# Gated MLP in three chunks of inner features, with seven block products for eight in five of eleven gate groups

## The chip, the cores and the metric

One core of one Trainium2 chip runs the kernel. The metric is device time in microseconds (us) for one execution. The kernel before was run three times: 2100.64 us is the median, 2100.33 the lowest and 2100.79 the highest. One further execution was profiled; its own time is 2100.51 us, and the span from its first to its last instruction is 2098.7 us.

In the profile, PE is the matrix engine (TensorE) and PEld its loads of the stationary operand. DVE is VectorE, ACT is ScalarE, POOL is GpSimd, and SP issues the DMAs. Each engine takes its own instructions in the order in which the program issues them.

## The reference

Two decoder layers on 256 tokens with 2048 features, all in float32. Layer 0 mixes tokens with MoBA attention, layer 1 with latent attention (MLA); each is followed by the gated MLP that the change is about:

```python
D_FF = 5632          # 44 tiles of 128 inner features
def conv_glu_ffn(h, w_gate, w_up, conv_w, conv_b, w_down):
    g = h @ w_gate                       # 256 x 2048 times 2048 x 5632
    g = causal_depthwise_conv(g, conv_w) + conv_b      # width 3 over tokens
    return (silu(g) * (h @ w_up)) @ w_down             # 5632 x 2048 back

x = x + mixer(rms_norm(x, attn_norm[i]))
x = x + conv_glu_ffn(rms_norm(x, ffn_norm[i]), ...)
```

(The convolution is written here as a function of that name; the reference calls a general one with one group per feature.)

## The kernel before

**Products in three parts.** Every weight is read as float32 and split into a high part, rounded to the matrix engine's format, and a low part that holds the rest. Activations are kept split in the same way. A product is then three matmuls: high by high, high by low, low by high (lines 261 to 263 in `feat_major`, line 235 in `tok_major`).

**Pieces and units.** A piece is 128 partitions by 512 weight columns. In the MLP a piece holds four tiles of 128 x 128, so 12 matmuls with 256 moving columns (the tokens). A unit is what one DMA brings, normally four pieces, 1 MB; three buffers named `raw` hold units. The list `units` fixes their order for the whole kernel. `Stream.split` makes the two parts of a piece: `whi` by a copy on ACT (line 104), then `wlo` by a subtraction on DVE (line 105). There are five buffers for each part.

**The order of the work is written out by hand.** `add` appends one quantum per piece. `at(q, f)` hangs a side step on quantum q, `first(q, f)` puts a step ahead of it. The loop at the end of `trunk` issues, for every q: the steps of `first`, then the splits up to piece q + 3, then the matmuls of piece q, then the side steps of q. So on DVE and on ACT the splits and the side steps stand in one line, and a side step that waits holds up every split behind it. Piece i can be split when piece i - 5 has left its buffer.

**The MLP before.** `plan_gate_up` goes through the 44 tiles of inner features; each tile is four gate pieces, then four up pieces. The side steps of a tile (class `FTile`) follow its gate product: `evac_gate` (DVE, line 675) takes it out of PSUM, `conv_last` (ACT, 682) and `conv_rest` (DVE, two operations of line 688) do the convolution, `silu` (ACT, 693), `scaled` (DVE, 696). After the up product come `product` (DVE, 699), `high` (ACT, 702) and `low` (DVE, 706), which leave the tile in `ffn["a"]`, with room for all 44. `plan_down_feat` then makes 16 output tiles of 11 pieces each, and `residual` (DVE, line 345) adds each to `xT`. After the down products of layer 0 the steps of the next norm hang on the same passes (lines 279, 284, 298, 302).

In `feat_major` the weight tile is stationary and the tokens move, so a result has features on partitions. In `tok_major` the activations are stationary and the weights move.

Of the kernel before, what the change touches and what calls it, by code (L numbers as in the profile page):

```python
# [10 lines left out]
F32 = mybir.dt.float32  # L11
F32R = mybir.dt.float32r
# [5 lines left out]
P = 128  # L18
# [30 lines left out]
BY_TOKEN, BY_FEATURE = (8, 8), (24, 56)  # L49

H_START = 8


class Stream:
# [3 lines left out]
    def __init__(self, nc, raw_pool, part_pool, units, starts):  # L58
        self.starts = starts
        self.nc, self.raw_pool, self.part_pool = nc, raw_pool, part_pool  # L60
        self.units = units
        self.pieces = [(u, i, n) for u, (_, k, n) in enumerate(units) for i in range(k)]
        self.raw, self.parts = {}, {}
        self.loaded = self.split_to = 0

    def load(self, upto):
        while self.loaded < min(upto, len(self.units)):
            u = self.loaded
            src, k, n = self.units[u]
            t = self.raw_pool.tile([P, 4 * 512], F32, name="raw")  # L70
            self.nc.sync.dma_start(t[:, : k * n], src)
            self.raw[u] = t
            self.loaded += 1

    def begin(self, load_x):

        ends = (2, 2, 3, 4, 6, 6, 8, 8, 10, 10, 13, 16)
        load_x(0, 1)
        at = 1
        for u in range(AHEAD_UNITS):  # L80
            src, k, n = self.units[u]
# [8 lines left out]
        self.loaded = AHEAD_UNITS  # L90

    def split(self, upto):
        while self.split_to < min(upto, len(self.pieces)):
# [3 lines left out]
            w = self.raw[u][:, j * n : (j + 1) * n]  # L97
            b, c = self.starts(u, j)
            hi = self.part_pool.tile([P, 512 + ROOM], F32R, name="whi")[:, b : b + 512]
            lo = self.part_pool.tile([P, 512 + ROOM], F32R, name="wlo")[:, c : c + 512]  # L100
            if i == 0:
                self.nc.vector.tensor_copy(hi[:, :n], w)
            else:
                self.nc.scalar.copy(hi[:, :n], w)  # L104
            self.nc.vector.tensor_tensor(  # L105
                lo[:, :n], w, hi[:, :n].bitcast(F32), op=ALU.subtract
            )
# [8 lines left out]
def trunk(ctx: ExitStack, tc: tile.TileContext, a, out):  # L116
# [14 lines left out]
    def units_of(name, n=512):  # L131
        w = a[name]
        return [(w[u], w.shape[2] // n, n) for u in range(w.shape[0])]

    def grouped(name, per, g):
        return units_of(name)[g * per : (g + 1) * per]
# [6 lines left out]
    units += units_of("ffn_gu0")  # L143
    units += units_of("ffn_down0")
    units += units_of("mla_wq_a")
    units += grouped("mla_wqr", 1, 0)
    units += units_of("mla_wkv_a", KVN)
# [6 lines left out]
    units += units_of("ffn_gu1")  # L154
    units += units_of("ffn_down1")
    def starts(u, j):

        return BY_TOKEN if u < 48 or 200 <= u < 222 else BY_FEATURE

    assert len(units) == 370  # L160
    ws = Stream(nc, raw_pool, part_pool, units, starts)
# [490 lines left out]
    def open_ffn(layer):  # L652
# [6 lines left out]
        ffn["a"] = ffn["pool"].tile([P, NF, 2 * S], F32R, name="a", bufs=1)  # L659
# [4 lines left out]
    class FTile:  # L664
        def __init__(self, layer, j, norm):
            self.layer, self.j, self.norm = layer, j, norm
            self.gate, self.up = {}, {}

# [32 lines left out]
        def high(self):  # L701
            nc.scalar.copy(ffn["a"][:, self.j, :S], self.c)

        def low(self):
            a_ = ffn["a"]
            nc.vector.tensor_tensor(
                a_[:, self.j, S:], self.c, a_[:, self.j, :S].bitcast(F32), op=ALU.subtract
            )

    def plan_gate_up(layer, norm):  # L710
        for j in range(NF):
            f = FTile(layer, j, norm)
            for kind, st in (("g", f.gate), ("u", f.up)):
# [3 lines left out]
                if kind == "g":  # L717
                    if j == 0:
                        at(q, open_ffn, layer)
                    at(q, f.evac_gate)  # L720
                    at(q + 1, f.conv_last)
                    at(q + 2, f.conv_rest)
                    at(q + 3, f.silu)
                    at(q + 4, f.scaled)
                else:
# [3 lines left out]

    plan_gate_up(0, n2)  # L730

    n3 = Norm(C_AN + KD, False)

    def plan_down_feat(norm):
        for j in range(KD):
            st = {}
            for kq in range(NF // 4):
                q = add(lambda t_hi, t_lo, n, st=st, kq=kq: feat_major(
                    st, lambda: ffn["a"], 4 * kq, NF - 1, kq == 0, t_hi, t_lo, n))
            at(q, residual, st, j, 0)  # L740
            if norm is None:
                at(q, store, j)
            elif j < KD - 1:
                norm.plan(q + 2, j)
            else:
                at(q, norm.now, j)
                at(q + 3, norm.sums)
        return q

    plan_down_feat(n3)  # L750
# [224 lines left out]
    plan_gate_up(1, n4)  # L975

    plan_down_feat(None)
# [125 lines left out]
```

## Time and profile before

| | us |
|---|---|
| median of three runs | 2100.64 |
| lowest, highest | 2100.33, 2100.79 |
| profiled execution, its own time | 2100.51 |
| its span | 2098.7 |
| PE busy in the span | 2090.2 |
| DVE busy | 1389.4 |
| ACT busy | 1134.2 |

How to read it: the span runs from the first to the last instruction. Busy time of an engine leaves out waits and the issuing of DMAs. Matmuls overlap, so the time that one takes (276 ns for 256 columns) is not the time from one to the next; that is read from the starts in the timeline. In a timeline row the columns are start, duration, engine, line, operation, output and inputs, count, and in brackets the idle time before it with what ended it. In a group row they are line, engine, operation, shapes and count, then total busy us and mean ns of one, then the idle time ahead.

Layer 0's MLP runs from about 393 to 1112 us of the span, and layer 1's from about 1376 us to the end.

### The profile page before, as it was taken

To read this page: it belongs to the slowest core of one execution; us is meant where nothing else is said; L and a number is where in the kernel's file an instruction comes from. 1 tells how busy PE (TensorE), PEld (TensorE's weight loads), DVE (VectorE), ACT (ScalarE), POOL (GpSimd) and SP (SyncE) were. 2 spreads that over 40 slices of the span, in tenths; PEclk is the share of its full clock that TensorE was granted. 3 is DMA by queue.
4 is the path that set the end of the run, shared out by engine and by line. 5 is a ranking of instruction groups with operands and counts; after the bars stand their busy time and mean duration, and the time that the engine had idled before them with its cause. 6 is when DMAs were issued, how large, how long until landed. Compare 5 with 4: busy or idle time off the path is not lost.

```text
span 2098.7 us, 42064 instructions
## 1 busy us (share of the span) xinstructions
PE 2090.2 (100%) x16684; PEld 2014.8 (96%) x16684; DVE 1389.4 (66%) x3036; ACT 1134.2 (54%) x2206; POOL 45.6 (2%) x37
## 2 busy tenths in 40 slices
PE   9999999999999999999999999999999999999999
PEld 7888889999999999999999889999999999999999
DVE  6776666766666766655556786767766667655554
ACT  6555555655555555545455675655555555544443
POOL 0000000000000000000000110000000000000000
PEclk9999999999999999999999999999999999999999
DMA  7444445555555555555554533545555555555553
GB/s 272 161 166 176 168 170 188 190 191 201 190 193 201 187 196 199 192 195 195 195 192 158 176 139 106 196 181 200 186 197 198 187 199 195 189 205 208 194 206 131
DMA packets 59381, 391.81 MB, mean 187 GB/s; under 512 B 6960, under 2 KB 10032, under 8 KB 13232
## 3 DMA queue, kind: packets, MB, share of 16 engines
q1 hardware_dynamic: 59040, 388.87, 52.3%
q8 instruction: 130, 2.13, 0.4%
q14 instruction: 67, 0.55, 0.1%
q10 hardware_dynamic: 144, 0.26, 0.1%
HBM read 387.01 MB, written 2.10 MB: 185 GB/s over the span
## 4 chain that ended last, share of the span: by engine, by line
PE 97%; DVE 1%; DMA 1%; issue 0%; ACT 0%; POOL 0%; SPq 0%; ACTq 0%; POOLq 0%
PE acc L261 26%; PE acc L263 26%; PE acc L262 26%; PE acc L235 15%; PE sc L473 1%; PE tp L449 1%; DMA raw<-in_moba_wq 1%; PE sc L520 1%; PE tp L509 0%; PE sc L476 0%; PE sc L521 0%; DVE wlo L105 0%; DMA xT<-in_xT 0%; DVE junk L379 0%; POOL hr L392 0%
## 5 line engine op out<-in xcount | busy, mean ns | idle before, releaser
L105 DVE TENSOR_TENSOR wlo<-raw,whi 128x512 fp32r<-128x512 f32 (+1 forms) x1480 | 1000.5, 684 | 424.6 <-ACT whi L104 422.5
L104 ACT CAST whi<-raw 128x512 fp32r<-128x512 f32 (+1 forms) x1479 | 871.8, 614 | 461.4 <-PE acc L262 213.6
L261 PE MATMUL acc<-h,whi 128*128 128x256 f32 x2880 | 795.3, 276 | 0.0
L263 PE MATMUL acc<-h,wlo 128*128 128x256 f32 x2880 | 794.9, 276 | 0.0
L262 PE MATMUL acc<-h,whi 128*128 128x256 f32 x2880 | 794.9, 276 | 0.0
L262 PEld LDWEIGHTS acc<-h,whi 128*128 128x128 f32 x2880 | 540.7, 188 | 0.0
L261 PEld LDWEIGHTS acc<-h,whi 128*128 128x128 f32 x2880 | 540.6, 188 | 0.0
L263 PEld LDWEIGHTS acc<-h,wlo 128*128 128x128 f32 x2880 | 540.6, 188 | 0.0
L261 PE MATMUL acc<-a,whi 128*128 128x256 f32 x1408 | 388.6, 276 | 0.0
L262 PE MATMUL acc<-a,whi 128*128 128x256 f32 x1408 | 388.6, 276 | 0.0
L263 PE MATMUL acc<-a,wlo 128*128 128x256 f32 x1408 | 388.6, 276 | 0.0
L235 PE MATMUL acc<-whi,h 128*128 128x512 f32 (+1 forms) x896 | 279.8, 385 | 0.7 <-ACT whi L104 0.5
L261 PEld LDWEIGHTS acc<-a,whi 128*128 128x128 f32 x1408 | 264.3, 188 | 0.0
L262 PEld LDWEIGHTS acc<-a,whi 128*128 128x128 f32 x1408 | 264.3, 188 | 0.0
L263 PEld LDWEIGHTS acc<-a,wlo 128*128 128x128 f32 x1408 | 264.3, 188 | 0.0
L235 PEld LDWEIGHTS acc<-whi,h 128*128 128x128 f32 x896 | 164.7, 188 | 31.5 <-ACT h L279 1.3
L235 PE MATMUL acc<-wlo,h 128*128 128x512 f32 (+1 forms) x448 | 169.3, 378 | 0.3 <-DVE wlo L105 0.2
L261 PE MATMUL acc<-oT,whi 128*128 128x256 f32 x512 | 144.8, 283 | 0.0
L263 PE MATMUL acc<-oT,wlo 128*128 128x256 f32 x512 | 141.7, 277 | 0.0
L262 PE MATMUL acc<-oT,whi 128*128 128x256 f32 x512 | 141.6, 277 | 0.0
L675 DVE TENSOR_TENSOR g<-acc,rstd_b 128x256 f32<-128x256 f32 x88 | 37.5, 426 | 126.0 <-PE acc L263 123.1
L682 ACT ACTIVATE c<-g,par 128x256 f32<-128x256 f32 x88 | 53.1, 603 | 108.1 <-DVE g L675 108.1
(141 smaller groups left out, 1558.0 us busy)
## 6 DMA issues: line engine op xcount, KB each, us to landing
raw<-in_ffn_gu SPq DMA_DIRECT2D x176, 1024.0 KB, 4.8
raw<-in_ffn_down SPq DMA_DIRECT2D x88, 1024.0 KB, 4.8
raw<-in_moba_wk SPq DMA_DIRECT2D x16, 1024.0 KB, 4.8
raw<-in_moba_wv SPq DMA_DIRECT2D x16, 1024.0 KB, 4.8
raw<-in_moba_wo SPq DMA_DIRECT2D x16, 1024.0 KB, 4.8
raw<-in_mla_wo SPq DMA_DIRECT2D x16, 1024.0 KB, 4.8
raw<-in_moba_wq SPq DMA_DIRECT2D x13, 1024.0 KB, 4.8
raw<-in_mla_wkv_a SPq DMA_DIRECT2D x8, 576.0 KB, 3.7
```

What stands on the lines that cost most here:

```text
L104: self.nc.scalar.copy(hi[:, :n], w)
L105: self.nc.vector.tensor_tensor(lo[:, :n], w, hi[:, :n].bitcast(F32), op=ALU.subtract)
L235: mm(state["acc"][t][:, :n], src[:, kt, c : c + P], (t_lo if part == 1 else t_hi)[:, :n], start=kt == 0 and part == 0, stop=kt == k_last a ...
L261: mm(o, w_hi, src[:, kt, :S], start=first and k == 0, stop=False, skip_group_check=True)
L262: mm(o, w_hi, src[:, kt, S:], start=False, stop=False, skip_group_check=True)
L263: mm(o, w_lo, src[:, kt, :S], start=False, stop=kt == k_last, skip_group_check=True)
L449: nc.tensor.transpose(tp[:, (i * NT + t) * P : (i * NT + t + 1) * P], flat[:, t, c : c + P], ident)
L473: mm(o, qT[:, i, q0 : q0 + P], kT[:, i, :n], start=True, stop=self.rope is None)
L520: mm(o[:, :S], v[:, 0, vs], self.pT[:, :S], start=True, stop=False)
L675: nc.vector.tensor_tensor(self.g[:, 2:], self.gate["acc"][:, :S], self.norm.rstd_b, op=ALU.mult)
L682: nc.scalar.activation(self.c, self.g[:, 2:], AF.Identity, bias=par[:, cb : cb + 1], scale=self.cw(2))
```

## The change

The MLP's 44 tiles are taken in three chunks: tiles 0 to 15, 16 to 31 and 32 to 43. After the gate and up products of a chunk, its down products are made at once: 16 passes of 4, 4 and 3 pieces, each with its own `residual`. `ffn["a"]` holds one chunk instead of 44 tiles.

For the five groups of four tiles named in `SUMS` (3, 4, 5, 8 and 9) the gate product is made by seven block products instead of eight. Tokens are cut into two halves and pairs of 128 input features into two, and the weights correspondingly; sums and differences of blocks are multiplied and combined. For a group there are four "sums" units, each of four tiles by 512 input features, and each unit is seven pieces of 6 matmuls with 256 moving weight columns and a stationary 128 x 128 block of activations. Four of the seven pieces of a unit are differences of weight blocks, made by `Stream.sum` on DVE in front of the split. The differences of the activations are made once per layer by `token_sums`, eight steps placed three pieces apart at the start of the MLP, and kept in `ffn["hs"]`. `joined` combines the seven results of a group, and `turned` brings each of its four tiles back to features on partitions by two transposes, just ahead of that tile's up pieces. The tile's steps from `evac_gate` to `scaled` then hang on the four up pieces.

The sums units of group 3 stand among the gate and up entries of the first chunk, one after every second tile; those of groups 4 and 5 stand among the down passes of chunk 0, and those of 8 and 9 among those of chunk 1, one after every second pass. The tiles 12 to 15, 16 to 23 and 32 to 39 thus have only up pieces in their place.

```diff
+CHUNKS = ((0, 16), (16, 32), (32, 44))
+SUMS = (3, 4, 5, 8, 9)
+def ffn_order():
+    order = []
+    def weave(plain, groups, begin, step):
+        sums = [("s", g, r) for g in groups for r in range(4)]
+        for i, p in enumerate(plain):
+            order.append(p)
+            if sums and i + 1 >= begin and (i + 1 - begin) % step == 0:
+                order.append(sums.pop(0))
+    for c, (j0, j1) in enumerate(CHUNKS):
+        plain = []
+        for j in range(j0, j1):
+            plain += [("p", j, kind) for kind in ("u" if j // 4 in SUMS else "gu")]
+        weave(plain, [3] if c == 0 else [], 8, 4)
...
+        weave([("d", c, j) for j in range(KD)], ahead, 2, 2)
...
+    def sum(self, upto):
+        while self.summed_to < min(upto, len(self.pieces)):
+            u, j, _ = self.pieces[self.summed_to]
+            self.summed_to += 1
+            if self.units[u][3] != "sums" or j in (0, 2, 4):
+                continue
+            if j == 3:
+                t = self.block(u, 1)
+                a, b = t, self.block(u, 0)
+            else:
+                t = self.sum_pool.tile([P, 512], F32, name="tsum", bufs=3)
...
+                if j == 1:
+                    a, b = self.block(u, 3), self.block(u, 1)
+                elif j == 5:
+                    a, b = self.block(u, 3), self.sums[u, 3]
+                else:
+                    a, b = self.block(u, 2), self.sums[u, 5]
+            self.sums[u, j] = t
+            self.nc.vector.tensor_tensor(t, a, b, op=ALU.subtract)
...
     def split(self, upto):
         while self.split_to < min(upto, len(self.pieces)):
...
             self.load(u + AHEAD_UNITS)
-            w = self.raw[u][:, j * n : (j + 1) * n]
+            self.sum(i + 1)
+            w = self.source(i)
...
-                self.nc.scalar.copy(hi[:, :n], w)
-            self.nc.vector.tensor_tensor(
-                lo[:, :n], w, hi[:, :n].bitcast(F32), op=ALU.subtract
-            )
+                self.nc.scalar.copy(w_hi, w)
+            if i + 1 < len(self.pieces) and self.pieces[i + 1][0] < self.loaded:
+                self.sum(i + 2)
+            self.nc.vector.tensor_tensor(w_lo, w, w_hi.bitcast(F32), op=ALU.subtract)
...
+    class Sums:
+        def work(self, norm, r, m, t_hi, t_lo, n):
...
+            for i in range(2):
...
+                mm(o, hi, w_hi, start=opens and i == 0, stop=False, skip_group_check=True)
+                mm(o, hi, w_lo, start=False, stop=False, skip_group_check=True)
+                mm(o, lo, w_hi, start=False, stop=last, skip_group_check=True)
+        def joined(self):
...
+            nc.scalar.copy(p1, w[:, :S])
...
+            add_(two(c[:, : 2 * S]), two(x[:, :]), twice(p1), op=ALU.add)
+            add_(two(f[:, :]), two(y[:, :]), twice(c[:, S : 2 * S]), op=ALU.add)
+            add_(c[:, 3 * S :], y[:, :S], f[:, S:], op=ALU.add)
+            add_(c[:, S : 3 * S], z[:, :], f, op=ALU.add)
+        def turned(self, tile_, i):
+            tile_.gate["acc"] = bank = ps_acc.tile([P, 512], F32, name="acc")
+            for t in range(NT):
+                at_ = t * 2 * S + i * P
+                nc.tensor.transpose(bank[:, t * P : (t + 1) * P], self.c[:, at_ : at_ + P], ident)
+    def token_sums(norm, pair):
...
+        for k in range(2):
+            c = norm.gain_col + 2 * pair + k
+            nc.scalar.activation(
+                x[:, k], xT[:, 2 * pair + k, :], AF.Copy, scale=par[:, c : c + 1]
+            )
...
+        sub(s_[:, 0], a21, a22, op=ALU.add)
+        sub(s_[:, 2], a11, a21, op=ALU.subtract)
+        sub(s_[:, 1], s_[:, 0], a11, op=ALU.subtract)
+        sub(s_[:, 3], a12, s_[:, 1], op=ALU.subtract)
...
+        nc.scalar.copy(hi, flat)
+        nc.vector.tensor_tensor(lo, flat, hi.bitcast(F32), op=ALU.subtract)
+    def plan_ffn(layer, norm, after):
...
+                for m in range(7):
+                    q = add(lambda t_hi, t_lo, n, grp=grp, r=r, m=m: grp.work(norm, r, m, t_hi, t_lo, n))
+                if r == 3:
+                    at(q, grp.joined)
...
+                    for pair in range(KD // 2):
+                        at(q + 4 + 3 * pair, token_sums, norm, pair)
+                if kind == "u" and j // 4 in SUMS:
+                    q0 = q - 4
+                    first(q0 + 1, groups[j // 4].turned, f, j % 4)
+                if kind == "g" or j // 4 in SUMS:
+                    at(q0, f.evac_gate) if kind == "g" else at(q0 + 1, f.evac_gate)
+                    at(q0 + 1, f.conv_last)
+                    at(q0 + 2, f.conv_rest)
+                    at(q0 + 3, f.silu)
+                    at(q0 + 4, f.scaled)
+                if kind == "u":
                     at(q, f.product)
                     at(q + 1, f.high)
                     at(q + 2, f.low)
```

The weights lie in memory as before. A sums unit is read as four runs of 2 KB per partition, and a down unit of a chunk by one or two DMAs of 1 to 4 pieces.

More of the change, by code (lines that the diff above doesn't have):

```diff
@@ L153, in trunk @@
     units += units_of("mla_wo")
[L154 to L161, printed above, removed]
+    units += ffn_units(1)
+    ws = Stream(nc, raw_pool, part_pool, units)
     att = ExitStack()
@@ L667, in __init__ @@
             self.gate, self.up = {}, {}
+            self.slot = j - max(j0 for j0, _ in CHUNKS if j0 <= j)
         def cw(self, i):
@@ L701, in high @@
         def high(self):
-            nc.scalar.copy(ffn["a"][:, self.j, :S], self.c)
+            nc.scalar.copy(ffn["a"][:, self.slot, :S], self.c)
         def low(self):
@@ L716, in plan_gate_up @@
                         st, lambda: norm.h, 4 * kq, KD - 1, kq == 0, t_hi, t_lo, n))
[L717 to L725, printed above, removed]
+                q0 = q
+                if kind == "g" and j == 0:
+                    at(q, open_ffn, layer)
+                    for pair in range(KD // 2):
[10 more added lines that the diff above has]
+                if kind == "u":
                     at(q, f.product)
```

177 lines of the change are left out of this document (135 added, 42 removed).

## Prediction

> **What bounds the kernel now.** I read the page first, then the matrix engine's share of the stretch that is layer 0's MLP, then the timeline of its matmuls, and last those of DVE and ACT in one tile, because the change trades matmuls for work there. The page, and the busy time of each engine from 393 to 1111 us:
>
> ```profile
> span 2098.7 us, 42064 instructions
> PE 2090.2 (100%) x16684; PEld 2014.8 (96%) x16684; DVE 1389.4 (66%) x3036; ACT 1134.2 (54%) x2206; POOL 45.6 (2%) x37
> PEclk9999999999999999999999999999999999999999
> ```
> ```profile
> core 0: us, PE busy (x) PEld busy (x) DVE busy (x) ACT busy (x) POOL busy (x), PEclk, DMA share, GB/s
> 393.00:1111.00 718.00, 718.00 (x6336) 717.90 (x6336) 470.52 (x845) 378.80 (x696) 1.08 (x1) 1.00 0.55 194
> ```
>
> PE is busy for 718.00 of 718.00 us there, at a granted clock of 1.00: no wait reaches it in the whole MLP. The pace is read from starts, here with 51 matmuls between the two rows:
>
> ```profile
> 600.05 0.28 PE L261 MATMUL acc<-h,whi 128*128 128x256 f32 x1
> ...
> 605.83 0.28 PE L261 MATMUL acc<-h,whi 128*128 128x256 f32 x1
> ```
>
> 5.78 / 51 = 113.3 ns. A piece of 12 matmuls is 1.36 us, four pieces 5.44, a sums piece of six 0.68. DVE's 66% looks like room, but a share hides the order. This is a tile before the change, first DVE, then ACT:
>
> ```profile
> 703.95 0.42 DVE L675 TENSOR_TENSOR g<-acc,rstd_b 128x256 f32<-128x256 f32 x1 [1.43 <-PE acc L263]
> 704.29 0.68 DVE L105 TENSOR_TENSOR wlo<-raw,whi 128x512 fp32r<-128x512 f32 x1
> 705.56 0.69 DVE L105 TENSOR_TENSOR wlo<-raw,whi 128x512 fp32r<-128x512 f32 x1 [0.58 <-ACT whi L104]
> 706.17 1.00 DVE L688 SCALAR_TENSOR_TENSOR c<-g,par,c 128x256 f32<-128x256 f32 x2
> 707.08 0.69 DVE L105 TENSOR_TENSOR wlo<-raw,whi 128x512 fp32r<-128x512 f32 x1
> 708.16 0.69 DVE L105 TENSOR_TENSOR wlo<-raw,whi 128x512 fp32r<-128x512 f32 x1 [0.39 <-ACT whi L104]
> 708.77 0.42 DVE L696 TENSOR_TENSOR c<-c,rstd_b 128x256 f32<-128x256 f32 x1
> 709.39 0.42 DVE L699 TENSOR_TENSOR c<-c,acc 128x256 f32<-128x256 f32 x1 [0.20 <-PE acc L263]
> 709.73 0.68 DVE L105 TENSOR_TENSOR wlo<-raw,whi 128x512 fp32r<-128x512 f32 x1
> ```
> ```profile
> 704.41 0.60 ACT L682 ACTIVATE c<-g,par 128x256 f32<-128x256 f32 x1 [1.26 <-DVE g L675]
> 704.92 1.13 ACT L104 CAST whi<-raw 128x512 fp32r<-128x512 f32 x2
> 707.20 0.42 ACT L693 ACTIVATE c<-c 128x256 f32<-128x256 f32 x1 [1.16 <-DVE c L688]
> 707.52 1.35 ACT L104 CAST whi<-raw 128x512 fp32r<-128x512 f32 x2
> ```
>
> See how the two engines wait for each other in turn: `conv_last` (L682) waits for `evac_gate`, the next `whi` stands behind it on ACT, DVE idles 0.58 us for that `whi`, and likewise around `silu` (0.39 us). That chain costs nothing today because a tile has 10.88 us (96 matmuls) for it.
>
> **The change part by part.**
>
> *Matmuls saved.* A group took 4 x 16 x 3 = 192, and now takes 28 pieces x 6 = 168. Ten groups: 240 x 113.3 ns = -27.2 us. No row has 256 weight columns moving; the nearest are the 512-wide ones at the end of the norm's passes:
>
> ```profile
> 1133.99 0.40 PE L235 MATMUL acc<-whi,cqT 128*128 128x512 f32 x1
> 1134.22 0.40 PE L235 MATMUL acc<-wlo,cqT 128*128 128x512 f32 x1
> 1134.46 0.62 PE L235 MATMUL acc<-whi,cqT 128*128 128x512 f32 x2
> 1134.92 0.39 PE L235 MATMUL acc<-wlo,cqT 128*128 128x512 f32 x1
> 1135.15 0.61 PE L235 MATMUL acc<-whi,cqT 128*128 128x512 f32 x2
> ```
>
> Five take 1.16 us from the switch, 232 ns each, against twice 113.3 = 227. I take 113.3; at half of 232 the 1680 sums matmuls add at most 4.5 us.
>
> *Transposes.* `turned` puts two among the matmuls, forty times. The nearest row is two transposes in the same stream:
>
> ```profile
> 398.62 0.28 PE L263 MATMUL acc<-h,wlo 128*128 128x256 f32 x1
> 398.80 0.43 PE L336 MATMUL tp<-ident,rstd 128*128 128x128 f32 x2
> 398.99 0.37 PE L261 MATMUL acc<-h,whi 128*128 128x256 f32 x1
> 399.19 0.28 PE L262 MATMUL acc<-h,whi 128*128 128x256 f32 x1
> ...
> 400.13 0.28 PE L261 MATMUL acc<-h,whi 128*128 128x256 f32 x1
> ```
>
> From 398.62 to 400.13 are ten matmuls, 1.13 us, and 1.51 passed: 0.38, of which 0.07 was a wait ahead of them. So 0.31 us, with 0.20 instead of 0.113 at the first matmul and 5 ns on each of the next: PE starts slowly after that break. I take it that it does so after a wait too and add 0.12 us to each stall below; without it the sums units' term falls by 4.8.
>
> *Tiles with only up pieces.* Twenty a layer do in four pieces, 5.44 + 0.31 = 5.75 us, what had 10.88. Their whole chain, start to start, in the order of issue: `product` to `wlo` 0.34, to `evac_gate` 0.61, its end 0.46, `conv_last` to the next `whi` 0.51, `whi` to `wlo` 0.64, `wlo` to `low` 0.61, `low` to `conv_rest` 0.34, both to `wlo` 0.91, to `silu` 0.12, to `whi` 0.32, to `wlo` 0.64, `wlo` to `scaled` 0.61, `scaled` to the next `product` 0.46. All from the fences above. The sum is 6.57 us, 0.82 more than PE needs and 1.13 more than the 5.44 it replaces. In the runs of eight (tiles 16 to 23, 32 to 39) nothing is in hand at the start, for a sums unit and `joined` stand ahead: 16 x 1.13 = 18.1 us a layer. The run of four (12 to 15) starts with three pieces in hand, some 3 us, against 4 x 0.82 = 3.3: it pays its transposes and 0.3, 1.5 us. Two layers: +39.2. The other end is a chain wholly hidden: 40 x 0.31 = +12.4.
>
> *`token_sums`.* Its prices, and those of a split:
>
> ```profile
> L105 DVE TENSOR_TENSOR wlo<-raw,whi 128x512 fp32r<-128x512 f32 x1448 | 987.3, 689 | 417.5 <-ACT whi L104 415.4
> L104 ACT CAST whi<-raw 128x512 fp32r<-128x512 f32 x1447 | 859.2, 618 | 455.8 <-PE acc L262 213.6 <-DVE wlo L105 199.6 <-PE acc L235 34.2
> L279 ACT ACTIVATE h<-xT,par 128x256 fp32r<-128x256 f32 x64 | 32.5, 509 | 18.4 <-DVE xT L345 13.2 <-DMA xT<-in_xT 5.1
> L435 DVE TENSOR_TENSOR ro<-qk,tab 128x128 f32<-128x128 f32 x16 | 4.7, 292 | 0.5
> ```
>
> Two ACT operations like L279 (0.41 to the next start, then 0.51 and 0.04 hand-over), four 128-wide DVE operations of which the third and fourth wait for one before (0.21 + 0.21 + 0.33 + 0.33), a 512-wide copy on ACT (0.66 with its hand-over), a subtraction on DVE (0.61): 3.3 us of chain in which no `wlo` is made. Every 4.08 us (three pieces) needs this, three `wlo` (1.82), three eighths of a tile's other DVE work (0.34 x 4 + 0.91 = 2.27, so 0.85) and about 0.3 of hand-over waits. That is 6.3, less the 0.4 in which the first ACT operation runs beside a `wlo`: 5.9, 1.8 too many, eight times 14.4 a layer. Of the lead of three pieces about 1.7 is free (a tile's own chain uses the rest), so 12.7, +25.4 in both layers. Bounds: 0, if it fits the idle gaps, and 2 x 8 x 2.2 = 35.
>
> *The sums units.* Seven splits and four differences, 11 DVE operations in 4.76 us. DVE operations overlap a little:
>
> ```profile
> 902.51 0.42 DVE L345 TENSOR_TENSOR xT<-xT,acc 128x256 f32<-128x256 f32 x1 [1.49 <-PE acc L263]
> 902.85 1.28 DVE L105 TENSOR_TENSOR wlo<-raw,whi 128x512 fp32r<-128x512 f32 x2
> ```
>
> Two `wlo` end within 1.28 us, so 0.60 from start to start (0.61 in the tile above). The unit follows a down pass, and its first three pieces are split before `residual`, which waits for the pass. Count from PE's first sums matmul: `residual` at 0.20 (as L675 follows its product), `wlo` 3 at 0.54, difference 1.15, `wlo` 4 1.75, difference 2.36, `wlo` 5 2.97, done 3.70 with hand-over. PE wants it at 5 x 0.68 + 0.11 = 3.51: a stall of 0.19 + 0.12 = 0.30. Piece 6 then just fits. 32 units: +9.6. In chunk 0 `low` stands in the line too: 0.34 more, 8 x 0.64 = +5.1. The differences read runs of 128 weights, which no row does on its own; by L435 four separate 128-wide operations hold DVE 0.84 instead of 0.61, and three such steps lie on this path: +0.7 a unit, 28 us at that end. I take the 512-wide row.
>
> *Costed at nothing.* The 64 added `residual` operations: DVE idles 1.49 us before one today; without that cover 0.34 each, 22 us. `joined`: 3.3 us behind its last product, covered by three ready pieces (4.08); uncovered, 33 us over ten. The end of a chunk: `low` of the last tile is due three or two pieces later. The loads, all on SP's queue:
>
> ```profile
> raw<-in_ffn_gu SPq DMA_DIRECT2D x176, 1024.0 KB, 4.8
> ```
>
> 4.8 us from issue to landing, and each is issued two units ahead, at least 10.2 us. Two DMAs for a down unit, or 2 KB runs, would have to double that.
>
> *Sum*: -27.2 + 39.2 + 25.4 + 14.7 = +52.1. The profiled execution took 2100.51 (span 2098.7; 1.8 lie around it), 0.1 below the median, so 2152.6; I say 2153.
>
> The Trainium skill's "VectorE: DVE Perf Modes", section Terms, says that a drain follows every DVE operation and that the next cannot issue until the pipe is empty. The row of two `wlo` in 1.28 us speaks against it for independent operations; by that rule the sum is the third rival's.
>
> **The rivals.**
>
> *Faster.* The three pieces of lead hide every chain. It is decided by one number: a tile with only up pieces must turn round in 5.75 us on DVE and ACT, not 6.57. Then -27.2 + 12.4, and no stalls: 2086. For it speak idle DVE of 1.43 us in the tile above and the 66%. Against it: that idle is gone when the period halves.
>
> *`token_sums` hidden.* They fall into gaps of ACT and DVE: 2153 - 25 = 2127. For it: the stretch is only 33 us a layer, and 417.5 us of idle stand before L105. Against: they are waits, not spare slots, and every step of `token_sums` hands over too.
>
> *Operations on DVE don't overlap*, 0.69 for 0.61: six places in a tile's chain (0.5 us, 32 tiles, 16) and six in a sums unit (0.5, 40 units, 20): 2189. *Runs of 128 are slow*: 2181.
>
> **How the numbers follow.** The three added terms together: 0.70. `token_sums` hidden: 0.12. Slow runs of 128: 0.09; no overlap: 0.03. Faster: 0.06. The range, 2122 to 2188, reaches from just below the second rival to the top of the third. A measurement of this kernel tells about 0.2% (4 us) from no change. Faster by more 0.06, within 0.02, slower 0.92.
>
> **What would show it.** 240 fewer matmuls and 80 more transposes; starts in the sums pieces 113 ns apart. Tiles 16 to 23 about 6.6 us apart, with `product` no longer waiting for PE but for `scaled`, and PE idle on `whi` and `wlo`. Stalls of one to two us from the second tile to the first sums unit. A stall near 0.3 us at the sixth piece of each sums unit between down passes, and none in the plain down passes or the tiles with gate pieces. The prediction is wrong if PE stays as full as it is now, or if the stalls stand at DMAs.

## The result, and the profile after

The changed kernel takes 2165.6 us (2164.95 to 2166.0) where the kernel before, measured beside it, takes 2100.53 (2100.33 to 2100.79): a ratio of 1.0309, 95% interval 1.0292 to 1.0327. It is 65.1 us slower. The page of the profiled execution, first the span and the engines, then the chain of work that ended last:

```profile
span 2164.1 us, 42508 instructions
PE 2127.2 (98%) x16524; PEld 2023.7 (94%) x16524; DVE 1605.1 (74%) x3500; ACT 1218.9 (56%) x2384; POOL 45.6 (2%) x37
PE 84%; DVE 10%; issue 3%; ACT 2%; DMA 0%; SPq 0%; POOL 0%; ACTq 0%; DVEq 0%; POOLq 0%
```

PE has 160 instructions fewer (240 matmuls less, 80 transposes more) and is busy 98% instead of 100%. Before, the chain was 97% PE and 1% DVE; now DVE holds 10% of it. No DMA stands in it. Yet DVE is busy for only 74% of the span. The next view is three windows of layer 0's MLP, with columns as in the prediction's window: the start of the MLP, where `token_sums` runs; a run of tiles with only up pieces; and a run of tiles with gate and up pieces.

```profile
410.00:446.00 36.00, 30.21 (x239) 28.02 (x239) 28.22 (x69) 22.19 (x47) 0.00 (x0) 1.00 0.44 150
725.00:759.00 34.00, 32.06 (x259) 30.06 (x257) 24.65 (x51) 18.07 (x37) 0.00 (x0) 1.00 0.44 158
790.00:824.00 34.00, 34.00 (x302) 34.00 (x302) 23.98 (x45) 18.01 (x36) 0.00 (x0) 1.00 0.54 189
```

In the second window DVE is busy 24.65 us and ACT 18.07, in the third 23.98 and 18.01: the same load. In the third PE is full with 302 matmuls; in the second it starts 259. What differs is not how much DVE and ACT do but how often they must hand a tile to each other.

To say where the 65.1 us lie I took every matmul start in the two MLPs, subtracted 113.3 ns from the distance to the next start, and added up what was left by kind of entry. The transposes are not counted as starts, so what they cost is part of this excess. It is used for all kernels below (us, both layers). The column of up-only tiles takes in all tiles from 12 on: the chain of a run's last up-only tile holds up the gate pieces of the tile behind it (tiles 24 and 40, 1.12 to 1.15 us each, 4.6 in all).

| | tiles 0 to 11 | 8 sums units of group 3 | up-only tiles | down passes | 32 sums units between passes | all |
|---|---|---|---|---|---|---|
| after | 20.8 | 14.3 | 39.1 | 3.9 | 15.8 | 93.9 |

The kernel before has 1.7 us of excess at the start of its two MLPs. So 93.9 - 1.7 - 27.2 (240 matmuls saved) = 65.0, which is the whole loss.

**Up-only tiles.** This is one of them, DVE first, then ACT:

```profile
738.82 0.69 DVE L189 TENSOR_TENSOR wlo<-raw,whi 128x512 fp32r<-128x512 f32 x1 [1.24 <-ACT whi L186]
...
739.76 1.00 DVE L789 SCALAR_TENSOR_TENSOR c<-g,par,c 128x256 f32<-128x256 f32 x2
740.68 0.68 DVE L189 TENSOR_TENSOR wlo<-raw,whi 128x512 fp32r<-128x512 f32 x1
741.75 0.69 DVE L189 TENSOR_TENSOR wlo<-raw,whi 128x512 fp32r<-128x512 f32 x1 [0.39 <-ACT whi L186]
742.36 0.42 DVE L797 TENSOR_TENSOR c<-c,rstd_b 128x256 f32<-128x256 f32 x1
742.88 0.42 DVE L800 TENSOR_TENSOR c<-c,acc 128x256 f32<-128x256 f32 x1
...
745.48 0.69 DVE L189 TENSOR_TENSOR wlo<-raw,whi 128x512 fp32r<-128x512 f32 x1 [1.24 <-ACT whi L186]
```
```profile
737.67 0.60 ACT L783 ACTIVATE c<-g,par 128x256 f32<-128x256 f32 x1 [0.59 <-DVE g L776]
738.18 1.12 ACT L186 CAST whi<-raw 128x512 fp32r<-128x512 f32 x2
740.79 0.42 ACT L794 ACTIVATE c<-c 128x256 f32<-128x256 f32 x1 [1.49 <-DVE c L789]
741.12 1.13 ACT L186 CAST whi<-raw 128x512 fp32r<-128x512 f32 x2
743.34 0.41 ACT L803 CAST a<-c 128x256 fp32r<-128x256 f32 x1 [1.09 <-DVE c L800]
744.34 0.60 ACT L783 ACTIVATE c<-g,par 128x256 f32<-128x256 f32 x1 [0.59 <-DVE g L776]
```

From `conv_last` (L783) to the next `conv_last` 6.67 us pass. ACT waits 1.49 us for `conv_rest`, DVE waits 1.24 for the `whi` that stands behind `conv_last`, and so on in turn. `product` (L800) starts as `scaled` (L797) ends: it waits for that, not for PE, which had started that tile's last matmul at 738.63.

**`token_sums`.** The waits of the stretch from 410 to 455 us (total, times, longest):

```profile
ACT hs L888 <- DVE ssum L885: 10.3, 7, 1.9
DVE hs L889 <- ACT hs L888: 4.8, 7, 0.7
PEld acc L360 <- DVE wlo L189: 4.2, 6, 1.4
PEld acc L358 <- ACT whi L186: 3.7, 5, 1.2
```

The copy into `hs` waits up to 1.9 us on ACT for the four small DVE operations, and the next `whi` stands behind it; PE then waits for `whi` and `wlo`.

**Sums units.** One unit between down passes, first some of PE's rows, then DVE's:

```profile
611.52 0.28 PE L840 MATMUL sc<-whi,h 128*128 128x256 f32 x1
...
614.35 0.28 PE L840 MATMUL sc<-whi,hs 128*128 128x256 f32 x1
...
615.06 0.28 PE L840 MATMUL tp<-whi,hs 128*128 128x256 f32 x1
615.21 0.39 PE L841 MATMUL tp<-wlo,hs 128*128 128x256 f32 x1
615.43 0.28 PE L842 MATMUL tp<-whi,hs 128*128 128x256 f32 x1
```
```profile
612.06 0.69 DVE L189 TENSOR_TENSOR wlo<-raw,whi 128x512 fp32r<-128x512 f32 x1
612.66 0.68 DVE L168 TENSOR_TENSOR tsum<-raw 128x512 f32<-128x512 f32 x1
613.27 0.68 DVE L189 TENSOR_TENSOR wlo<-raw,whi 128x512 fp32r<-128x512 f32 x1
613.87 0.69 DVE L168 TENSOR_TENSOR tsum<-raw,tsum 128x512 f32<-128x512 f32 x1
614.47 0.68 DVE L189 TENSOR_TENSOR wlo<-tsum,whi 128x512 fp32r<-128x512 f32 x1
615.32 0.69 DVE L189 TENSOR_TENSOR wlo<-tsum,whi 128x512 fp32r<-128x512 f32 x1 [0.17 <-ACT whi L186]
```

Between the first two PE rows are 24 matmuls without a stall: 2.83 / 24 = 118 ns, not 113.3. At piece 6 (615.06) the second matmul, the first with `wlo`, comes 0.15 us after the first and the third 0.22 after that: the late `wlo` of 614.47. A difference (L168) takes 0.68 to 0.69 us, as a `wlo` does.

### The profile page after: what moved, and what is told of

Its sections match the earlier page's. It is cut to its first block, busy times and chain, and to the rows that moved or that the text cites. A ratio compares the mean times of both kernels' runs of the same rounds, so it can differ in the third digit from the quotient of the medians.

```text
span 2164.1 us, 42508 instructions
## 1 busy us (share of the span) xinstructions
PE 2127.2 (98%) x16524; PEld 2023.7 (94%) x16524; DVE 1605.1 (74%) x3500; ACT 1218.9 (56%) x2384; POOL 45.6 (2%) x37
## 4 chain that ended last, share of the span: by engine, by line
PE 84%; DVE 10%; issue 3%; ACT 2%; DMA 0%; SPq 0%; POOL 0%; ACTq 0%; DVEq 0%; POOLq 0%
PE acc L360 19%; PE acc L358 19%; PE acc L359 19%; PE acc L332 15%; DVE wlo L189 5%; PE tp L841 2%; PE tp L842 1%; PE tp L840 1%; PE sc L841 1%; ACT whi L186 1%; PE sc L842 1%; PE sc L840 1%; PE sc L570 1%; DVE c L789 1%; PE tp L546 1%
## 5 line engine op out<-in xcount | busy, mean ns | idle before, releaser
L189 DVE TENSOR_TENSOR wlo<-raw,whi 128x512 fp32r<-128x512 f32 (+1 forms) x1480 | 980.5, 681 | 268.9 <-ACT whi L186 266.5
L186 ACT CAST whi<-raw 128x512 fp32r<-128x512 f32 (+1 forms) x1479 | 860.5, 613 | 332.9 <-PE acc L359 214.7
L360 PE MATMUL acc<-h,wlo 128*128 128x256 f32 x2240 | 628.8, 281 | 16.6 <-DVE wlo L189 16.1
L358 PE MATMUL acc<-h,whi 128*128 128x256 f32 x2240 | 625.5, 279 | 4.7 <-ACT whi L186 4.7
L359 PE MATMUL acc<-h,whi 128*128 128x256 f32 x2240 | 620.1, 277 | 0.0
L360 PEld LDWEIGHTS acc<-h,wlo 128*128 128x128 f32 x2240 | 421.2, 188 | 31.0 <-DVE wlo L189 30.7
L358 PEld LDWEIGHTS acc<-h,whi 128*128 128x128 f32 x2240 | 421.5, 188 | 7.0 <-ACT whi L186 6.5
L359 PEld LDWEIGHTS acc<-h,whi 128*128 128x128 f32 x2240 | 421.6, 188 | 0.0
L442 DVE TENSOR_TENSOR xT<-xT,acc 128x256 f32<-128x256 f32 x128 | 52.4, 420 | 127.7 <-PE acc L360 127.6
L186 ACT CAST whi<-tsum 128x512 fp32r<-128x512 f32 x120 | 74.6, 622 | 108.7 <-DVE tsum L168 108.7
```

Source lines behind the costliest of these rows:

```text
L186: self.nc.scalar.copy(w_hi, w)
L189: self.nc.vector.tensor_tensor(w_lo, w, w_hi.bitcast(F32), op=ALU.subtract)
L358: mm(o, w_hi, src[:, kt, :S], start=first and k == 0, stop=False, skip_group_check=True)
L359: mm(o, w_hi, src[:, kt, S:], start=False, stop=False, skip_group_check=True)
L360: mm(o, w_lo, src[:, kt, :S], start=False, stop=kt == k_last, skip_group_check=True)
L442: nc.vector.tensor_tensor(xT[:, j, :], xT[:, j, :], state["acc"][:, half * S : (half + 1) * S], op=ALU.add)
```

## The experiments

The theory after the result: PE loses its time at three places where DVE and ACT turn round too slowly for it, each by the order of their work: `token_sums`, the up-only tiles, and the differences in the sums units. The rivals: the chunks themselves (more `residual`s, split loads) cost; DVE or ACT is simply full; or removing a stall only moves it to the next place. All kernels compute the whole reference. The kernels with one edit ran twice each, the chunks alone eight times, the others five or six times; the runs of one kernel lie within 2.5 us.

### The chunks alone

```diff
-SUMS = (3, 4, 5, 8, 9)
+SUMS = ()
...
-                    for pair in range(KD // 2):
-                        at(q + 4 + 3 * pair, token_sums, norm, pair)
```

> No group in sums: SUMS is empty, token_sums and their tile are gone, all 44 gate tiles are plain again. What is left of the change is the three chunks, with 16 passes of 4, 4 and 3 pieces and 64 more residual operations. Theory (costed at nothing in the prediction): within 2 us of before, 2099 to 2103. Rival (the chunks cost, by the residual operations, the wait at a chunk's end or the smaller loads): 64 x 0.34 = 22 us more at most, 2122.

Measured 2100.39 us (2099.98 to 2100.63), ratio 0.9999 (0.9987 to 1.001). Its page:

```profile
span 2098.5 us, 42189 instructions
PE 2089.6 (100%) x16684; PEld 2014.9 (96%) x16684; DVE 1405.3 (67%) x3100; ACT 1133.3 (54%) x2206; POOL 45.6 (2%) x37
```

64 more `residual`s on DVE and smaller loads cost nothing that can be measured. Everything lost belongs to the five groups.

### `token_sums` spread evenly

```diff
-                        at(q + 4 + 3 * pair, token_sums, norm, pair)
+                        at(q + 4 + 10 * pair, token_sums, norm, pair)
```

> The eight token_sums steps of a layer stand ten pieces apart instead of three; nothing else changes, every operation is still made. Theory (a chain of hand-overs between ACT and DVE that is too long for its period): ten pieces last 13.6 us, the chain and the splits in them about 13, so the stalls between the second tile and the first sums unit go, 2165.6 - 26 = 2140 us, and the first sums unit costs no more than the three after it. Rival (DVE and ACT simply have too much to do there): the work only moves, and no more than 5 us are gained, 2160 to 2165.

Measured 2156.29 us (2155.98 to 2156.61), ratio 1.0264 (1.0234 to 1.0294): some 9 us back, not 25. Two windows, the old place of `token_sums` and a later one:

```profile
405.00:436.00 31.00, 31.00 (x276) 31.00 (x275) 25.17 (x54) 19.09 (x38) 0.00 (x0) 1.00 0.50 172
464.00:480.00 16.00, 13.93 (x102) 13.32 (x102) 13.15 (x26) 9.31 (x18) 0.00 (x0) 0.89 0.50 172
```

PE is full where it had stalled; the tiles' excess falls from 20.8 to 5.0. But now steps fall into the second and third sums unit of group 3, whose differences already stand in DVE's line; the excess of group 3's units rises from 14.3 to 21.0 (0.84 to some 3.2 and 3.8 us in the second and third). Of the 15.8 us that the tiles gave back, 6.7 came again there: the rival that the work only moves was right in part, and the expectation had not counted what stands beside the new places. The 0.89 in the second window is the granted clock, on which the last section has more.

### `token_sums` clear of the sums units

```diff
-                        at(q + 4 + 3 * pair, token_sums, norm, pair)
+                        at((7, 17, 40, 46, 63, 69, 86, 92)[pair] + q - 3, token_sums, norm, pair)
```

> The eight token_sums steps stand at pieces 7, 17, 40, 46, 63, 69, 86 and 92 of the MLP, each after a sums unit has ended and at least five pieces before the next one begins; all else is as in the changed kernel. In the run with ten pieces between them the stalls of tiles 1 to 3 were gone, but the steps had fallen into or just ahead of the second and third sums unit, which then lost 2.4 and 2.9 us more each. Theory (hand-over chain; it costs only where the lead of three pieces is short): both are gone, 2165.6 - 26 = 2140 us. Rival (the work of token_sums must be paid wherever it stands): as with ten pieces, 2156.

Measured 2143.03 us (2142.7 to 2143.36), ratio 1.0204 (1.0185 to 1.0222): 22.6 us back. The window that had lost most:

```profile
405.00:436.00 31.00, 31.00 (x275) 31.00 (x275) 25.55 (x52) 19.02 (x37) 0.00 (x0) 1.00 0.53 194
```

The tiles' excess is 2.3 (1.7 of it was there before the change), that of group 3's units 10.1. The same eight steps on the same engines cost little where they stand apart from each other and from the differences. So their place was the cost. The 3 us missing to the expectation lie in the three later units of group 3, at 1.4 us each instead of 0.84. A step stands nine pieces ahead of each of them, and fifteen ahead of the first, which stays at 0.84; that the distance makes the difference was not tested alone.

### The up-only tile's steps one piece apart

```diff
+                if late:
+                    at(q0 + 1, f.evac_gate)
+                    at(q0 + 2, f.conv_last)
+                    at(q0 + 3, f.conv_rest)
+                    at(q0 + 4, f.silu)
+                    at(q0 + 5, f.scaled)
...
-                    at(q, f.product)
-                    at(q + 1, f.high)
-                    at(q + 2, f.low)
+                    at(q + late, f.product)
+                    at(q + 1 + late, f.high)
+                    at(q + 2 + late, f.low)
```

(`late` is 1 for a tile with only up pieces, else 0; in the changed kernel `evac_gate` and `conv_last` hang on the same piece.)

> In the tiles with only up pieces, conv_last, conv_rest, silu, scaled, product, high and low are each hung one piece later, so that no step on ACT or DVE is issued before its forerunner on the other engine is done. Same operations, same pieces. Theory (the turn-round of the chain, 6.6 us a tile, is the bound): the tile falls to 5.44 + 0.24 = 5.7 us, 40 tiles, about -32 us: 2134. Rival (DVE's amount of work in those stretches is the bound): no operation is gone, so the time stays within 5 us of 2165.6. Second rival (the transposes and the slow start behind them are the cost): no change either.

Measured 2140.46 us (2140.05 to 2140.87), ratio 1.0189 (1.0159 to 1.0218): 25 us back with no operation removed, only each step of the chain hung one piece after the one that it waits for. Two windows of the first run of eight tiles, its first half and its second:

```profile
715.00:735.00 20.00, 20.00 (x179) 20.00 (x178) 16.59 (x34) 10.85 (x22) 0.00 (x0) 1.00 0.46 165
735.00:759.00 24.00, 23.74 (x202) 23.07 (x202) 19.31 (x41) 13.67 (x29) 0.00 (x0) 1.00 0.50 174
```

Four tiles run at 5.68 us, with PE full; the next four at 5.87 to 6.07. The excess of the up-only tiles falls from 39.1 to 16.7. Of that 40 x 0.24 = 9.6 are the transposes (measured below), so some 7 us of stalls stay, which the expectation did not have. They come of the same chain, which the edit made shorter, but not short enough. Two of ACT's rows in the second window:

```profile
740.60 0.60 ACT L783 ACTIVATE c<-g,par 128x256 f32<-128x256 f32 x1
746.67 0.60 ACT L783 ACTIVATE c<-g,par 128x256 f32<-128x256 f32 x1
```

`conv_last` now follows `conv_last` after 6.07 us, not 6.67, but PE needs 5.68. The same 6.07 us pass in the first window (728.47 to 734.53), where PE is still fed from the pieces split ahead; after four tiles these are used up. DVE's busy share is no sign of it: 83% (16.59 of 20 us) where PE is full, 80% (19.31 of 24) where it stalls.

### Up-only tiles mixed with full tiles

```diff
+        ups = [j for j in range(j0, j1) if j // 4 in SUMS]
+        both = [j for j in range(j0, j1) if j // 4 not in SUMS]
+        per = {8: 1, 4: 2}.get(len(both), 0) if c else 0
+        order_ = []
+        while per and both:
+            order_ += ups[:per] + both[:1]
+            ups, both = ups[per:], both[1:]
-        for j in range(j0, j1):
+        for j in order_ + both + ups:
```

> The entries of chunks 1 and 2 change places: a tile with only up pieces is followed by one with gate and up pieces (chunk 1), or two such by one (chunk 2). No operation is added, removed or hung elsewhere. Theory (6.6 us of turn-round against a period of 5.7 us): a pair now has 16.3 us for two chains, or three chains have 21.8 us, so the 18 us a layer of the two runs of eight fall to the transposes, 0.24 a tile: about -32 us + 2 for chunk 0, which stays, 2136. Rival (the up-only tiles cost DVE time wherever they stand): unchanged, 2160 to 2166.

Measured 2140.9 us (2140.65 to 2141.16), ratio 1.0194 (1.0175 to 1.0212). A window over most of the first mixed run:

```profile
728.00:836.00 108.00, 108.00 (x955) 108.00 (x954) 81.35 (x158) 60.05 (x119) 0.00 (x0) 1.00 0.53 197
```

PE is full for 108 us. The steps' order within a tile is as in the changed kernel; a full tile between two up-only ones gives back the lead of three pieces. The excess of the up-only tiles falls from 39.1 to 13.7, of which 9.6 are again the transposes; most of the other 4 us lies at the head of the runs (tile 24's gate pieces lose 0.6 us, tile 40's 1.1), and the expectation had left it out. Two edits that share no line give the same 25 us: the place was named rightly.

### The differences made a unit ahead

```diff
+            if self.units[u][3] != "sums" and u + 1 < len(self.units) and self.units[u + 1][3] == "sums":
+                self.difference(u + 1, (1, 3, 5, 6)[j])
```

(in `split`, behind the `wlo` of each piece of the unit ahead; the two calls of `sum` there go, and `difference` holds the same four subtractions.)

> The four differences of weight blocks of a sums unit are made one by one behind the four splits of the unit ahead of it, instead of among its own seven splits. Same operations. Theory (DVE falls behind inside the unit, eleven operations in 4.76 us): the stalls at the sixth and seventh piece go, 0.28 us in each of 32 units and 0.64 in each of 8, about -14 us: 2152. Rival (the loss is in the switch of orientation on PE): within 2 us of 2165.6. What is left of a unit's excess, about 0.2 us, is pace: its matmuls start 118 ns apart and not 113, and neither theory says that this changes.

Measured 2152.97 us (2152.79 to 2153.16), ratio 1.0248 (1.0218 to 1.0278). DVE in a sums unit of this kernel:

```profile
611.44 1.29 DVE L180 TENSOR_TENSOR wlo<-raw,whi 128x512 fp32r<-128x512 f32 x2
612.65 1.29 DVE L180 TENSOR_TENSOR wlo<-tsum,whi 128x512 fp32r<-128x512 f32 x2
613.88 2.81 DVE L180 TENSOR_TENSOR wlo<-raw,whi 128x512 fp32r<-128x512 f32 x4
```

Nothing stands between the `wlo` any more, and the stalls at pieces 6 and 7 are gone. The excess of a unit falls from 0.48 to 0.20 us, and this 0.20 is spread evenly, 0.03 in each of the seven pieces: 42 x 5 ns. That part is no stall; it is the pace of these matmuls. At the start of the MLP, where the differences now meet `token_sums`, tile 3's up pieces lose 4.17 us instead of 1.97, so the tiles' excess rises to 25.6.

### All four together

The edits of the last four headings in one kernel.

> Four edits together: token_sums clear of the sums units, the later steps in tiles with only up pieces, the mixed entries, the differences behind the splits of the unit ahead. Theory: what is left of the loss is 40 x 0.24 for the transposes = 9.6 us, 40 sums units x 0.23 for their pace of 118 ns = 9.2, and some 3 us of remains; against the 27.2 saved that is 2100.5 - 5.4 = 2095, a little faster than before. Rival (some of the stalls have another cause than the order): above 2105.

Measured 2107.27 us (2106.07 to 2108.49), ratio 1.0033 (1.0021 to 1.0045): 58 of the 65 us back, but not the gain that was expected. The excess of tiles 0 to 11 is 2.4, of the up-only tiles 8.8, of the units between passes 6.8. Group 3's units went up to 16.0: some 1.2 us in the first of a layer, 2.2 in the others. What PE waits for in ten microseconds (465 to 475) around the second of them, its weight loads first among the waits:

```profile
PEld tp L841 <- DVE wlo L187: 1.4, 4, 0.7
```

Group 3's units stand among tiles with gate pieces, so four differences made ahead now fall into the same splits as a tile's own steps and a `token_sums`. With the differences ahead alone the three later units keep 0.20 us each, with `token_sums` clear alone 1.40, with both some 2.2: each edit had been right alone, and the two fill the same slots.

### Another column for the weight parts

In the kernel of the last heading, the two parts of the sums pieces start at columns (24, 56) instead of (56, 24) of their buffers, to see whether the pace of 118 ns hangs on that.

```diff
-STARTS = {"token": (8, 8), "feature": (24, 56), "sums": (56, 24)}
+STARTS = {"token": (8, 8), "feature": (24, 56), "sums": (24, 56)}
```

> The same with one more edit: the parts of a sums piece start at columns 24 and 56 of their buffers instead of 56 and 24. Theory A (the 118 ns of the sums matmuls come from where their operands lie): another pace, up to 113 ns, 8 us less, 2087. Theory B (the pace is that of the switch from the other orientation and of a stationary load that never gets ahead): the same pace and time as the run beside it, 2095.

Measured 2107.05 us (2106.63 to 2107.43), ratio 1.0032 (1.002 to 1.0045). A unit between passes keeps 0.19 us of excess, spread as before. Not that.

### Four groups instead of five

Group 3, the only one whose units stand among gate pieces, is made plainly; `token_sums` gets the room up to the first unit of group 4; the other three edits stay.

```diff
-SUMS = (3, 4, 5, 8, 9)
+SUMS = (4, 5, 8, 9)
-        weave(plain, [3] if c == 0 else [], 8, 4)
+        weave(plain, [], 8, 4)
-                        at(q + 4 + 3 * pair, token_sums, norm, pair)
+                        at(q + 9 + 14 * pair, token_sums, norm, pair)
```

> The run with all edits lost 2.2 us in each of the sums units of group 3, which stand among tiles with gate pieces where DVE has the least to spare; the others lost 0.20. So group 3 is plain again here (SUMS is 4, 5, 8, 9; token_sums 14 pieces apart in the first chunk, which then holds no sums), with the same edits: late steps, mixed entries, differences ahead. Theory: saved 8 groups x 24 matmuls x 113.3 ns = 21.8 us; paid 32 x 0.24 for the transposes = 7.7, 32 x 0.23 for the pace of the sums units = 7.4; 2100.2 - 6.7 = 2093.5, faster than before by 0.3%. Rival (token_sums and the residuals of the three chunks still cost time): 2098 or more.

Measured 2094.42 us (2093.87 to 2095.29), ratio 0.997 (0.9959 to 0.9982), 6 us below the kernel before beside it (2100.39). The page, its chain, and the window of layer 0's MLP:

```profile
span 2093.1 us, 42482 instructions
PE 2084.0 (100%) x16556; PEld 2009.3 (96%) x16556; DVE 1576.0 (75%) x3436; ACT 1221.6 (58%) x2358; POOL 45.7 (2%) x37
PE 98%; DVE 1%; DMA 0%; issue 0%; ACT 0%; POOL 0%; SPq 0%; POOLq 0%; ACTq 0%
390.00:1108.00 718.00, 718.00 (x6303) 717.89 (x6302) 564.65 (x1045) 423.39 (x774) 1.08 (x1) 1.00 0.56 196
```

PE is busy for 718.00 of 718.00 us, while DVE, at 564.65, has 20% more to do than before (470.52). Saved are 192 x 113.3 ns = 21.8 us; the excess is 1.7 + 7.3 + 0.9 + 6.8 = 16.7, of which the pace of the sums matmuls is 32 x 0.20 = 6.4 and the transposes, by the 0.24 us measured below, 32 x 0.24 = 7.7. These two are the price that stays when nothing waits. By this sum (21.8 - 16.7 + 1.7) the MLPs gain 6.8 us; the medians say 6.0.

### Both operands at the other kinds' columns

The kernel of the last heading, with sums parts at (8, 8) and `hs` moved to column 8 of its tile.

```diff
-STARTS = {"token": (8, 8), "feature": (24, 56), "sums": (56, 24)}
+STARTS = {"token": (8, 8), "feature": (24, 56), "sums": (8, 8)}
...
+        hs = pool.tile([P, KD * 4 * P + 64], F32R, name="hs", bufs=1)
+        ffn["hs"] = hs[:, 8 : 8 + KD * 4 * P].rearrange("p (k a s) -> p k a s", k=KD // 2, a=2)
```

> The same, but the parts of a sums piece start at column 8 of their buffers, and the tile hs at column 8 of its own, as weights and h do in the products before the MLP that have the same orientation. Theory A (the 118 ns follow from where both operands lie together): up to 113 ns, 6 us less, 2087. Theory B (they do not): 2093.5, as the run beside it.

Measured 2093.89 us (2093.54 to 2094.04), ratio 0.9968 (0.9955 to 0.998). Two of its PE rows, 24 matmuls apart:

```profile
594.38 0.28 PE L841 MATMUL sc<-whi,h 128*128 128x256 f32 x1
...
597.22 0.28 PE L841 MATMUL sc<-whi,hs 128*128 128x256 f32 x1
```

2.84 / 24 = 118 ns, as before. Why weights that move past stationary activations go 4% slower than tokens that move past stationary weights stays open; where the operands lie did not change it. This kernel and the last one can't be told apart in time, and both are 0.3% faster than the kernel before.

The excess of all the stages, in one table (us, both layers):

| | tiles 0 to 11 | 8 sums units of group 3 | up-only tiles | down passes | 32 sums units between passes | all |
|---|---|---|---|---|---|---|
| after | 20.8 | 14.3 | 39.1 | 3.9 | 15.8 | 93.9 |
| `token_sums` spread | 5.0 | 21.0 | 39.4 | 3.6 | 15.9 | 84.9 |
| `token_sums` clear | 2.3 | 10.1 | 39.5 | 3.9 | 15.8 | 71.5 |
| steps a piece apart | 20.8 | 14.3 | 16.7 | 0.7 | 16.1 | 68.7 |
| tiles mixed | 20.8 | 14.3 | 13.7 | 3.5 | 16.0 | 68.4 |
| differences ahead | 25.6 | 8.1 | 35.4 | 5.1 | 6.8 | 80.9 |
| all four | 2.4 | 16.0 | 8.8 | 1.4 | 6.8 | 35.4 |
| four groups | 1.7 | - | 7.3 | 0.9 | 6.8 | 16.7 |

## Why the prediction was right, and by how much its terms missed

The forecast was 2153 us by a sum of +52.1; measured were 2165.6 and +65.0, inside the range. The mechanism was right at all three places. One term was clearly too small, and two others came out as closely as they did partly by luck.

- **Matmuls saved.** 240 fewer, 27.2 us at 113.3 ns. But the step that priced the matmuls with 256 moving weight columns failed: it took 113.3 ns, half of a 512-wide pair at most 116, and so at most 4.5 us. They start 118 ns apart, 0.20 us a unit, about 8 us in 40 units. This is the larger part of the 13 us that were missing, and no row of the trace before had the form; the row of 512 columns was no bound for it.
- **Sums units.** With the pace they cost 23.5 us (15.8, 8 x 0.84 = 6.7, and 1.0 in the passes behind them) for the 14.7 predicted; without the pace some 15. The stall of a unit between passes was 0.30 by the prediction and is 0.28, but that is partly luck. Predicted was one wait of 0.19 at the sixth piece and a slow start of 0.12 behind it, with the seventh just fit. The rows show two short waits, 0.03 at the sixth piece and 0.05 at the seventh, and a slow start of 0.10 behind each (615.21 to 615.43, and 616.07 to 616.29). For group 3's units 0.64 was predicted and 0.63 found.
- **Up-only tiles.** 6.57 us predicted for the turn-round, 6.59 to 6.72 measured for tiles 18 to 23, 6.67 in the rows above. The term was 39.2, measured 39.1 plus 2.9 (1.45 a layer) in the first down pass behind the run of four, which the prediction left out: the lead is used up when the passes begin. That 39.1 is so close is partly luck. The prediction gave the runs of eight no lead, but their first two tiles lose only 0.27 and 0.67 us of the 1.13 each, some 5.3 us less in the four runs; and it put nothing on the tiles with gate pieces, but tiles 24 and 40 lose the 4.6 us named above. The transposes cost less than taken:

```profile
565.85 0.28 PE L360 MATMUL acc<-h,wlo 128*128 128x256 f32 x1
565.97 0.38 PE L868 MATMUL acc<-ident,cs 128*128 128x128 f32 x2
...
567.22 0.28 PE L358 MATMUL acc<-h,whi 128*128 128x256 f32 x1
```

From 565.85 to 567.22 are ten matmuls, 1.13 us, and 1.37 passed: 0.24, not 0.31. Tiles 12 to 15, without a stall, run at 5.68 us.
- **`token_sums`.** 25.4 predicted; 20.8 - 1.7 in the tiles, and 2 x (4.63 - 0.84) = 7.6 for what the first sums unit of each layer has more than the others: 26.7.
- **Costed at nothing.** `residual`s, chunk ends and loads: the chunks alone took 0.9999 of the time before. The loads of the sums units, in runs of 2 KB, are not in that kernel; in the changed kernel no DMA stands in the chain. `joined` shows no stall of its own. Outside the places named, plain tiles and down passes run as before.
- **The rivals.** *Faster* needed a turn-round of 5.75 us. The changed kernel does not have it (6.67), and with the steps a piece apart it is still 6.07; PE keeps its 5.68 a tile only while the lead lasts. The number was the right one to ask for: with mixed entries as well (four groups) the tiles have more time than that, and PE is full. *`token_sums` hidden* fell with the 20.8. *No overlap on DVE*: in the rows of the sums unit operations of 0.68 to 0.69 us start 0.60 to 0.61 apart (612.06, 612.66, 613.27, 613.87). The rule of the Trainium skill's "VectorE: DVE Perf Modes", section Terms, that the next operation waits until the pipe is empty, is not borne out by them; the prediction's sum with it was 2189. *Slow runs of 128*: the differences take 0.68 to 0.69 us, the price of a `wlo`.

The experiments showed two of my later expectations wrong, those of `token_sums` spread evenly and of all four edits together, and for one reason: each was priced as if the other work stayed where it was. In both, the moved steps met the differences of group 3.

## What to carry to other kernels

Taking matmuls off a full matrix engine pays only if what replaces them turns round on the other engines within the shorter time that is left; compute that chain, hand-over by hand-over, instead of reading their busy share, which was 72% with PE starved and 79% with PE full. Hang each step one quantum after the one that it waits for, and alternate heavy entries with light ones: either edit gave back 25 us with the same operations. Price a matmul form that the trace does not show with a margin of some per cent per instruction, and when two fixes are joined, look which slots both of them fill.

## What the runs showed of the hardware that was not expected

- Matmuls with 128 x 128 activations stationary and 256 float32 weight columns moving start 118 ns apart, the mirrored form 113.3. Three placements of the weight parts and two of `hs` gave the same. The orientation alone does not explain it: in the changed kernel tokens that move past weights also start 0.83 us apart over seven matmuls behind a stall (741.64 to 742.47), 118 to 119 ns each, before they come back to 113.3; and the 512-wide form with activations stationary, 232 ns apart in the prediction's rows, goes on at 227 in the kernel before (1135.15 to 1136.51, six matmuls). The sums matmuls do not come back within their 42.
- After a pair of transposes in the stream 0.24 us are lost here, 0.31 by the row of before (its wait of 0.07 left out).
- The granted clock fell to half for 3.4 us at a time; the 0.89 of the window from 464 to 480 us is the mean over such a dip (474.8 to 478.2). The changed kernel has one in layer 1's `token_sums`:

```profile
1433.40:1436.80 3.40, 1.79 (x13) 1.40 (x12) 2.64 (x5) 2.25 (x6) 0.00 (x0) 1.00 0.42 176
1436.80:1440.20 3.40, 3.40 (x18) 3.40 (x17) 2.58 (x9) 1.58 (x5) 0.00 (x0) 0.50 0.27 41
```

Right before the dip PE is busy for 1.79 of 3.40 us, with no more than 1.5 us from one start to the next; in the dip 18 matmuls start instead of 30. Where an execution has several dips they lie whole multiples of 3.413 us apart. So I took the four traces that have dips in their MLPs (the changed kernel, `token_sums` spread, steps a piece apart, differences ahead) in stretches of 3.413 us counted from a dip. In the MLPs PE is busy for 48 to 54% of each of the seven stretches right ahead of a dip, and for 58% or more of every other one. Between 54 and 58% nothing was seen. A dip need not cost time: tiles 0 to 11 lose 20.8 us with none (tiles mixed), one (changed kernel) and two (steps a piece apart), where PE would have waited anyway; with `token_sums` spread, tile 6's gate pieces lose 1.43 us in layer 0, where the dip falls, and nothing in layer 1.
